# Sample state updates of a GLA decoder step: four masked fp32 matmuls replaced by four single-pass matmuls over stacked halves

## The chip, the cores and the metric

The kernel runs on one core of a Trainium2 chip. The metric is the device time of one execution in microseconds (us). Its engines are PE (matmuls), DVE, ACT and POOL (elementwise work) and SP, which here only issues transfers; ACT issues two as well.

## The reference, cut to what matters

Two layers of a decoder trunk: a half-step SwiGLU FFN, a mixer (gated linear attention beside a convolution, merged by gates), a second FFN. There are 336 token rows: a prompt of 256, 8 running sequences ("samples") of 8 tokens each, 16 meta tokens. The part at hand, for one head (dk = 128, dv = 256) and each of the 8 samples:

```
decay = jnp.exp(b_last[:, :, 0])
upd = jnp.einsum('bnshd,bnshv->bnhdv', k * jnp.exp(b_last - b), v)   # sum over the sample's 8 tokens
S_new = decay[..., None] * S + upd                                    # 128 x 256 per sample and head
```

Everything is float32 outside; large products are made of two fp32r halves ("hi" is the value rounded to fp32r, "lo" the rest).

## The kernel before, in words

All engines follow a hand-written order. The mixer of a layer runs projections, each a block of 8 steps of three matmuls `pgate` (about 3.7 us of PE with nothing between); after each step `tick()` emits one entry of a list `tasks`, so that small pieces of attention stand between the matmuls of the gate blocks. After the task, `tick` calls `fill()`, which emits one step of the depthwise convolution (31 taps for each of 8 channel blocks, one DVE operation on `acc` and one on `acs` a step) when the planner's estimate of DVE's work is more than 7000 ns behind that of PE's. The estimate of a matmul is four times as high for F32 operands as for F32R:

```
clock["pe"] += (n / 2.4 + 2.5) * (4 if b.dtype == F32 else 1)
...
if filler[0] is not None and clock["dve"] + 7000.0 < clock["pe"]:
```

The four heads take a list of 29 slots each (`head_tasks`): `prompt_out` at 0 and 3, `sample_out` at 7 to 13, `sample_state` at 15 and 18 (4 samples each), and at 21 to 23 `head_start` of the next head: scores, `mask_ku` on POOL, then `prompt_state`, whose first part is the update by the 16 meta tokens. What the convolution still owes is emitted at once when the third of the last eight gate blocks begins (`while next(conv, 0)`, block index 2). At the end of that block PE sums the squares of the convolution (`conv_norm_a`, tile `nrm` from `ones_d`), and from that the chain root, reciprocal (`rstd`), scaling, `ch`/`cl` leads to the pointwise projection `pw`.

Keys stand token by token in `kuT` (64 sample tokens in partitions 0 to 63, meta tokens in 64 to 79 of group 2). `mask_ku` writes `km`, eight copies of the keys, each zero outside one sample. `sample_state` then makes four F32 matmuls over 32 rows, two in each of two PSUM banks, and DVE adds them to the decayed state.

SP issues everything in one order: weight pieces `raw` (four buffers, each freed by POOL's or DVE's `wl`), old states `s` (three buffers), new states `out_ss`, prompt states `out_sp`. After each head stand out_ss, load of s, out_ss, load of s; a load of `s` waits until an `out_ss` ahead of it has landed, since it reuses its buffer. All matmuls of PE outside transposes are recorded at L134 (`mm`), nearly all DVE operations at L112.

Of the kernel before, what the change touches and what calls it, by code (L numbers as in the profile page):

```python
# [9 lines left out]
F32 = mybir.dt.float32  # L10
F32R = mybir.dt.float32r
U32 = mybir.dt.uint32
AF = mybir.ActivationFunctionType
ALU = mybir.AluOpType
# [6 lines left out]
NS = 8  # L21
LS = 8
NSAMP = NS * LS
# [6 lines left out]
HEADS = 4  # L30
DK = 128
DV = 256
# [10 lines left out]
NCH = SEQ // CHUNK  # L43
# [74 lines left out]
def trunk_kernel(ctx, tc, wts, x_in, vecs, consts, masks, wdecay, cache, state,  # L118
                 y_out, sp_out, ss_out, u_out):
    nc = tc.nc  # L120
    PE, ACT, POOL, SP = nc.tensor, nc.scalar, nc.gpsimd, nc.sync
# [5 lines left out]
    DVE = Clocked(nc.vector, dve_time)  # L127

    def mm(out, a, b, start, stop):
        n = 1  # L130
        for x in b.shape[1:]:
            n *= x
        clock["pe"] += (n / 2.4 + 2.5) * (4 if b.dtype == F32 else 1)
        PE.matmul(out, a, b, start=start, stop=stop)  # L134
# [21 lines left out]
    seqm = con[:, C_SEQ:C_SEQ + NS]  # L156
# [4 lines left out]
    def bank(name, tag="mm", bufs=4):  # L161
        return psum.tile([128, 512], F32, tag=tag, name=name, bufs=bufs)
# [4 lines left out]
    def grp(g):  # L167
        return slice(g * 128, (g + 1) * 128)
# [174 lines left out]
    def mixer(l, norm, next_block):  # L343
# [6 lines left out]
        gp = gl.enter_context(tc.tile_pool(name="gla", bufs=1, reuse_waits="tile"))  # L350
# [2 lines left out]
        lal = mp.tile([128, 3, 512], F32R, tag="sb", name="lal")  # L353
        qt = gp.tile([128, HEADS, T], F32, name="qt")
        kt = gp.tile([128, HEADS, TP], F32, name="kt")
        kuT = gp.tile([128, 4, HEADS * DK], F32, name="kuT")
        v = gp.tile([128, 3, HEADS * DV], F32, name="v")
        dec = gp.tile([128, HEADS, 2 * NCH + NS], F32, name="dec")
        rT = gp.tile([128, 3], F32, name="rT")
# [16 lines left out]
        ACT.copy(wds[0:64], wdec[0:64])  # L376
        ACT.copy(wdr[64:128], wdec[64:128])
        POOL.tensor_tensor(out=wds[64:128], in0=wdec[64:128], in1=wdr[64:128].bitcast(F32), op=ALU.subtract)
        POOL.memset(kuT[0:64, 3], 0.0)
        cnorm = Norm()  # L380

        ready = [0]
# [149 lines left out]
        at = {0: decay_lr, 6: decay_alr, 14: decay_exp, 18: decay_ln, 70: decay_end}  # L532
# [13 lines left out]
        for hd in range(HEADS):  # L546
# [3 lines left out]
                                     op0=ALU.mult, op1=ALU.mult)  # L550
            DVE.tensor_tensor(out=qt[:, hd, 0:n], in0=pq[:, 0:n], in1=qt[:, hd, 0:n], op=ALU.mult)

        def transposes(hd):
            pt = bank("ptr", "aux", 2)
            for g in range(3):
                PE.transpose(pt[:, grp(g)], ku[:, hd, grp(g)], ident)
                clock["pe"] += 108.0
            hs = slice(hd * DK, (hd + 1) * DK)
            ACT.copy(kuT[:, 0:3, hs], pt[:, :384].rearrange("p (g d) -> p g d", g=3))
            ACT.copy(kuT[64:128, 3, hs], pt[64:128, grp(2)])  # L560

        for hd in range(HEADS):
            pk = bank("pk")
# [25 lines left out]
        hp = gl.enter_context(tc.tile_pool(name="heads", bufs=1, reuse_waits="tile"))  # L589
        s0 = {}  # L590

        def load_s0(i):
            if i < 2 * HEADS:
                t = hp.tile([128, NS // 2, DV], F32, tag="s0", name="s0", bufs=3)
                SP.dma_start(t, state[l, i // 2, i % 2])
                s0[i] = t
# [4 lines left out]
        def scores(hd, st):  # L601
            ps = bank("sc")
            for g in range(3):
                e = min((g + 1) * 128, n)
                mm(ps[:, g * 128:e], kt[:, hd, grp(g)], qt[:, hd, g * 128:e], True, True)
            DVE.copy_predicated(probs[hd % 2].rearrange("p g c -> p (g c)")[:, :n], msk[:, :n], ps[:, :n])

        def prompt_state(hd, st, part):
            ks = slice(hd * DK, (hd + 1) * DK)
            vs = slice(hd * DV, (hd + 1) * DV)  # L610
            pu = bank("upd", "aux", 2)
            if part == 0:
                sp = st["sp"] = hp.tile([128, 2 * NCH, DV], F32, tag="sp", name="sp", bufs=1)
                mm(pu[:, 0:DV], kuT[:, 3, ks], v[:, 2, vs], True, True)
                ACT.activation(sp[:, 0], pu[:, 0:DV], AF.Identity, scale=dec[:, hd, 1:2])
                return
            sp = st["sp"]
            for g in range(NCH):
                mm(pu[:, g * DV:(g + 1) * DV], kuT[:, g, ks], v[:, g, vs], True, True)
            for g in range(NCH):  # L620
                if g:
                    ACT.activation(sp[:, 2 * g], sp[:, 2 * g - 1], AF.Identity, scale=dec[:, hd, 2 * g + 1:2 * g + 2])
                DVE.scalar_tensor_tensor(out=sp[:, 2 * g + 1], in0=sp[:, 2 * g], scalar=dec[:, hd, 2 * g:2 * g + 1],
                                         in1=pu[:, g * DV:(g + 1) * DV], op0=ALU.mult, op1=ALU.add)
            SP.dma_start(sp_out[l, hd], sp[:, 2 * NCH - 1])

        def prompt_out(hd, st, vb):
            sp = st["sp"]
            pr = probs[hd % 2]
            o = st["o", vb] = bank("o")  # L630
            vs = slice(hd * DV + vb * 128, hd * DV + (vb + 1) * 128)
            ss = slice(vb * 128, (vb + 1) * 128)
            for g in range(NCH):
                mm(o[:, grp(g)], v[:, g, vs], pr[:, g], True, False)
                mm(o[:, grp(g)], sp[:, 2 * g, ss], qt[:, hd, grp(g)], False, True)
            mm(o[:, SEQ:n], v[:, 2, vs], pr[:, 2, 0:n - SEQ], True, False)

        def mask_ku(hd, st):
            km = st["km"] = hp.tile([64, NS, DK], F32, tag="km", name="km", bufs=1)
            src = kuT[0:64, 2, hd * DK:(hd + 1) * DK]  # L640
            POOL.tensor_tensor(out=km, in0=src.unsqueeze(1).to_broadcast([64, NS, DK]),
                               in1=seqm[0:64].unsqueeze(2).to_broadcast([64, NS, DK]), op=ALU.mult)

        def sample_out(hd, st, half, vb):
            t = s0[2 * hd + half]
            for i in range(NS // 2):
                s = half * (NS // 2) + i
                cs = slice(SEQ + s * LS, SEQ + (s + 1) * LS)
                mm(st["o", vb][:, cs], t[:, i, vb * 128:(vb + 1) * 128], qt[:, hd, cs], False, s == NS - 1)

        def sample_state(hd, st, p):
            km = st["km"]
            pus = [bank("upds", "aux", 2) for _ in range(2)]
            for e in range(2):
                for half in range(2):
                    s = half * (NS // 2) + 2 * p + e
                    r = slice(32 * half, 32 * half + 32)
                    mm(pus[half][:, e * DV:(e + 1) * DV], km[r, s], v[r, 2, hd * DV:(hd + 1) * DV], True, True)
            for half in range(2):
                t = s0[2 * hd + half]  # L660
                for e in range(2):
                    i = 2 * p + e
                    s = half * (NS // 2) + i
                    DVE.scalar_tensor_tensor(out=t[:, i], in0=t[:, i], scalar=dec[:, hd, 2 * NCH + s:2 * NCH + s + 1],
                                             in1=pus[half][:, e * DV:(e + 1) * DV], op0=ALU.mult, op1=ALU.add)
            if p == 1:
                for half in range(2):
                    SP.dma_start(ss_out[l, hd, half], s0.pop(2 * hd + half))
                    load_s0(2 * hd + half + 3)

        def head_evict(hd, st):
            ot = st["ot"] = hp.tile([128, 2, T], F32, tag="ot", name="ot", bufs=1)
# [17 lines left out]
        hs = [{} for _ in range(HEADS)]  # L690

        def head_start(hd):
            st = hs[hd]
            return {0: lambda: (scores(hd, st), mask_ku(hd, st)), 1: lambda: prompt_state(hd, st, 0),
                    2: lambda: prompt_state(hd, st, 1)}

        def head_tasks(hd):
            st = hs[hd]
            at = {
                0: lambda: prompt_out(hd, st, 0),  # L700
                3: lambda: prompt_out(hd, st, 1),
                7: lambda: sample_out(hd, st, 0, 0),
                9: lambda: sample_out(hd, st, 0, 1),
                11: lambda: sample_out(hd, st, 1, 0),
                13: lambda: (sample_out(hd, st, 1, 1), head_evict(hd, st)),
                15: lambda: sample_state(hd, st, 0),
                18: lambda: sample_state(hd, st, 1),
            }
            if hd:
                at[5] = lambda: head_norm_a(hd - 1, hs[hd - 1])  # L710
                at[10] = lambda: head_norm_b(hd - 1, hs[hd - 1])
            if hd + 1 < HEADS:
                at.update({21 + k: f for k, f in head_start(hd + 1).items()})
            else:
                at[23] = lambda: head_norm_a(hd, st)
                at[28] = lambda: head_norm_b(hd, st)
            return [at.get(k) for k in range(29)]

        at = head_start(0)
# [87 lines left out]
    with tc.manual_schedule():  # L807
# [52 lines left out]
        r = norm.rstd(ones_d, TY)  # L860
        for b in range(KB):
            DVE.scalar_tensor_tensor(out=h[:, b, 0:TY], in0=h[:, b, 0:TY], scalar=vec[:, V_FIN + b:V_FIN + b + 1],
                                     in1=r[:, 0:TY], op0=ALU.mult, op1=ALU.mult)
# [121 lines left out]
```

## Time and profile before

| | |
|---|---|
| median of 3 runs | 1649.36 us (1649.2 to 1652.94) |
| the profiled execution's own time | 1653.15 us |
| its span in the trace | 1651.4 us |
| PE busy | 1615.1 us, 98% |
| DVE, ACT, POOL busy | 65%, 44%, 26% |
| granted PE clock, mean | 0.991 |

The span is what the trace covers, the own time has some 1.8 us around it. Times below are from the start of the span; layer 0's mixer lies at about 255 to 570 us, layer 1's at about 1078 to 1390 us.

### The profile page before, as it was taken

How to read it: one execution, taken by the hardware profiler on the slowest of the kernel's cores; microseconds unless marked ns; L12 is line 12 of the kernel's file. 1: busy time of each engine (PE TensorE's matmuls, PEld its weight loads, DVE VectorE, ACT ScalarE, POOL GpSimd, SP SyncE). 2: the span in 40 equal slices, each digit the busy share in tenths (PEclk: the TensorE clock that was granted, in tenths of full speed). 3: DMA queues.
4: the chain of work that ended last, by engine and by line, in shares of the span. 5: the costliest groups of instructions: out<-in, count | busy, mean ns of one | idle time of the engine just before them, and what ended most of it. 6: DMA issues, size and time to landing. Idle time of an engine off the chain costs nothing.

```text
span 1651.4 us, 27129 instructions
## 1 busy us (share of the span) xinstructions
PE 1615.1 (98%) x10612; PEld 1596.0 (97%) x10612; DVE 1080.0 (65%) x2159; ACT 727.6 (44%) x1154; POOL 424.7 (26%) x284
## 2 busy tenths in 40 slices
PE   8999999899999999999999999998999999999997
PEld 8999999899998999999999999998999989999997
DVE  7666446899986566564456654468998865666543
ACT  5433433743446344333343334347434464433432
POOL 0000016575575310000000000166756652000000
PEclk9999999999999999999999999999999999999999
DMA  5654445365453544444446444553644544445352
GB/s 200 203 181 126 133 152 163 112 182 166 131 173 115 154 140 153 141 130 141 152 142 212 141 134 131 157 150 112 192 156 142 173 136 151 148 153 153 116 171 78
DMA packets 76593, 247.56 MB, mean 150 GB/s; under 512 B 8625, under 2 KB 10929, under 8 KB 76209
## 3 DMA queue, kind: packets, MB, share of 16 engines
q1 hardware_dynamic: 75888, 240.34, 46.3%
q10 hardware_dynamic: 576, 5.49, 0.9%
q8 instruction: 83, 1.36, 0.3%
q14 instruction: 46, 0.37, 0.1%
HBM read 230.08 MB, written 15.71 MB: 149 GB/s over the span
## 4 chain that ended last, share of the span: by engine, by line
PE 85%; DVE 7%; ACT 4%; issue 2%; DMA 1%; POOL 0%; SPq 0%; DVEq 0%; POOLq 0%; ACTq 0%
PE pd L134 19%; PE pu L134 19%; PE pg L134 19%; PE pgate L134 6%; PE pw L134 4%; PE po L134 4%; DVE acc L112 2%; PE pa L134 2%; PE pga L134 2%; PE pv L134 2%; PE o L134 2%; PE pk L134 2%; PE pq L134 2%; DVE acs L112 1%; ACT wh L205 1%
## 5 line engine op out<-in xcount | busy, mean ns | idle before, releaser
L112 DVE TENSOR_TENSOR wl<-raw,wh 128x1024 fp32r<-128x1024 f32 (+1 forms) x320 | 349.3, 1108 | 228.1 <-ACT wh L205 227.6
L205 ACT CAST wh<-raw 128x1024 fp32r<-128x1024 f32 (+3 forms) x456 | 427.7, 956 | 74.4 <-issue 29.4
L207 POOL TENSOR_TENSOR wl<-raw,wh 128x1024 fp32r<-128x1024 f32 (+2 forms) x136 | 308.9, 2285 | 155.1 <-ACT wh L205 146.0
L270 POOL TENSOR_TENSOR ssum<-ssum,sq 128x336 f32<-128x336 f32 (+1 forms) x63 | 56.8, 901 | 1013.9 <-ACT sq L269 1013.8
L112 DVE SCALAR_TENSOR_TENSOR acc<-u,vec,acc 128x272 f32<-128x272 f32 (+1 forms) x480 | 235.2, 490 | 0.0
L134 PE MATMUL pg<-xh,wh 128*128 128x336 f32 (+1 forms) x704 | 222.8, 316 | 6.8 <-ACT wh L205 6.8
L134 PE MATMUL pg<-xh,wl 128*128 128x336 f32 (+1 forms) x704 | 221.8, 315 | 0.3 <-DVE wl L112 0.3
L134 PE MATMUL pu<-xh,wh 128*128 128x336 f32 (+1 forms) x704 | 221.6, 315 | 0.0
L134 PE MATMUL pu<-xh,wl 128*128 128x336 f32 (+1 forms) x704 | 221.6, 315 | 0.0
L134 PE MATMUL pd<-act_hi,wh 128*128 128x336 f32 (+1 forms) x704 | 221.0, 314 | 0.0
L134 PE MATMUL pu<-xl,wh 128*128 128x336 f32 (+1 forms) x704 | 220.9, 314 | 0.0
L134 PE MATMUL pg<-xl,wh 128*128 128x336 f32 (+1 forms) x704 | 220.9, 314 | 0.0
L134 PE MATMUL pd<-act_hi,wl 128*128 128x336 f32 (+1 forms) x704 | 220.3, 313 | 0.0
L134 PE MATMUL pd<-act_lo,wh 128*128 128x336 f32 (+1 forms) x704 | 220.2, 313 | 0.0
L134 PEld LDWEIGHTS pg<-xh,wh 128*128 128x128 f32 x704 | 132.7, 189 | 7.1 <-ACT wh L205 6.8
L112 DVE SCALAR_TENSOR_TENSOR acs<-u,vec,acs 128x64 f32<-128x64 f32 x480 | 135.5, 282 | 0.0
L326 ACT CAST act_hi<-pu 128x336 fp32r<-128x336 f32 (+1 forms) x88 | 38.5, 437 | 217.6 <-DVE pu L112 217.6
L134 PEld LDWEIGHTS pg<-xh,wl 128*128 128x128 f32 x704 | 132.6, 188 | 0.8 <-DVE wl L112 0.8
L134 PEld LDWEIGHTS pg<-xl,wh 128*128 128x128 f32 x704 | 132.7, 188 | 0.4
L134 PEld LDWEIGHTS pu<-xl,wh 128*128 128x128 f32 x704 | 132.6, 188 | 0.0
L134 PEld LDWEIGHTS pu<-xh,wl 128*128 128x128 f32 x704 | 132.6, 188 | 0.0
L134 PEld LDWEIGHTS pu<-xh,wh 128*128 128x128 f32 x704 | 132.6, 188 | 0.0
(200 smaller groups left out, 3277.4 us busy)
## 6 DMA issues: line engine op xcount, KB each, us to landing
raw<-in_wts SPq DMA_DIRECT2D x304, 512.0 KB, 3.6
raw<-in_wts SPq DMA_DIRECT2D x64, 384.0 KB, 3.6
raw<-in_wts SPq DMA_DIRECT2D x64, 320.0 KB, 3.0
s<-in_state SPq DMA_DIRECT2D x16, 512.0 KB, 4.5
out_ss<-s SPq DMA_DIRECT2D x16, 512.0 KB, 5.2
raw<-in_wts SPq DMA_DIRECT2D x16, 344.0 KB, 3.4
u<-in_cache ACTq DMA_DIRECT2D x2, 2424.0 KB, 11.0
out_u<-u SPq DMA_DIRECT2D x16, 303.0 KB, 4.6
```

What stands on the lines that cost most here:

```text
L112: return fn(*args, **kw)
L134: PE.matmul(out, a, b, start=start, stop=stop)
L205: ACT.copy(wh[:, :nk * nw], raw)
L207: eng.tensor_tensor(out=wl[:, :nk * nw], in0=raw, in1=wh[:, :nk * nw].bitcast(F32), op=ALU.subtract)
L270: eng.tensor_tensor(out=self.sum[:, 0:n], in0=self.sum[:, 0:n], in1=sq[:, 0:n], op=ALU.add)
L326: ACT.copy(ah[:, j, 0:n], pu[:, 0:n])
```

## The change: what it does

For each head, `sample_split` casts the head's 64 rows of keys and values to fp32r (`hi`, ACT) and subtracts (`lo`, POOL). `sample_stack` then issues twelve transfers inside SBUF on SP (32 rows of 512 to 1536 bytes, 16 to 48 KB each), which lay the four combinations hi·hi, hi·lo, lo·hi, lo·lo of the 8 tokens of a sample under each other: 32 rows of `kv` per sample, four samples in 128 partitions, two such halves. A sample's update is then one fp32r matmul over 32 rows with 256 columns, in a single pass. `mask_ku` and `km` go. The meta update reads 32 rows of `kuT` group 2 and `v` in place of a zero-padded fourth group of 128 rows, so the fourth group, its memset and its copy go. `head_start` stands one slot earlier (20), and the stacking at slot 25.

```diff
-            ACT.copy(kuT[:, 0:3, hs], pt[:, :384].rearrange("p (g d) -> p g d", g=3))
-            ACT.copy(kuT[64:128, 3, hs], pt[64:128, grp(2)])
+            ACT.copy(kuT[:, :, hs], pt[:, :384].rearrange("p (g d) -> p g d", g=3))
...
-                mm(pu[:, 0:DV], kuT[:, 3, ks], v[:, 2, vs], True, True)
+                mm(pu[:, 0:DV], kuT[NSAMP:NSAMP + 32, 2, ks], v[NSAMP:NSAMP + 32, 2, vs], True, True)
...
-        def mask_ku(hd, st):
-            km = st["km"] = hp.tile([64, NS, DK], F32, tag="km", name="km", bufs=1)
...
+        def sample_split(hd, st):
+            hi = st["hi"] = hp.tile([NSAMP, DK + DV], F32R, tag="hi", name="hi", bufs=1)
+            lo = st["lo"] = hp.tile([NSAMP, DK + DV], F32R, tag="lo", name="lo", bufs=1)
+            for o, w, raw in ((0, DK, kuT), (DK, DV, v)):
+                raw = raw[0:NSAMP, 2, hd * w:(hd + 1) * w]
+                ACT.copy(hi[:, o:o + w], raw)
+                POOL.tensor_tensor(out=lo[:, o:o + w], in0=raw, in1=hi[:, o:o + w].bitcast(F32), op=ALU.subtract)
+
+        def sample_stack(hd, st):
+            dst = st["kv"] = hp.tile([128, 2, DK + DV], F32R, tag="kv", name="kv", bufs=1)
+            hi, lo, ks, vs = st["hi"], st["lo"], slice(0, DK), slice(DK, DK + DV)
+            for r, part in enumerate((((hi, slice(0, DK + DV)),), ((hi, ks), (lo, vs)), ((lo, ks), (hi, vs)),
+                                      ((lo, slice(0, DK + DV)),))):
+                for t, cs in part:
+                    for e in range(2):
+                        SP.dma_start(dst[r:128:4, e, cs].bitcast(F32), t[32 * e:32 * e + 32, cs].bitcast(F32))
...
-                for half in range(2):
-                    s = half * (NS // 2) + 2 * p + e
-                    r = slice(32 * half, 32 * half + 32)
-                    mm(pus[half][:, e * DV:(e + 1) * DV], km[r, s], v[r, 2, hd * DV:(hd + 1) * DV], True, True)
...
+                for j in range(2):
+                    r = slice(32 * (2 * p + j), 32 * (2 * p + j) + 32)
+                    mm(pus[j][:, e * DV:(e + 1) * DV], st["kv"][r, e, 0:DK], st["kv"][r, e, DK:], True, True)
...
-            return {0: lambda: (scores(hd, st), mask_ku(hd, st)), 1: lambda: prompt_state(hd, st, 0),
+            return {0: lambda: (scores(hd, st), sample_split(hd, st)), 5: lambda: sample_stack(hd, st), 1: lambda: prompt_state(hd, st, 0),
...
-                at.update({21 + k: f for k, f in head_start(hd + 1).items()})
+                at.update({20 + k: f for k, f in head_start(hd + 1).items()})
```

SP's order in layer 0, from the second state store after head 1 to the weight pieces that follow (`s` are state buffers). Before:

```order
L668 DMA out_ss<-s_4510 128x1024
L595 DMA s_4775<-in_state 128x1024
L625 DMA out_sp<-sp 128x256
L192 DMA raw_4847<-in_wts 128x1024
L192 DMA raw_4906<-in_wts 128x1024
```

The same place now:

```order
L675 DMA out_ss<-s_4520 128x1024
L593 DMA s_4790<-in_state 128x1024
L623 DMA out_sp<-sp 128x256
L651 DMA kv<-hi 32x384 x2
L651 DMA kv<-hi 32x128 x2
L651 DMA kv<-lo 32x256 x2
L651 DMA kv<-lo 32x128 x2
L651 DMA kv<-hi 32x256 x2
L651 DMA kv<-lo 32x384 x2
L192 DMA raw_4865<-in_wts 128x1024
```

The twelve transfers of head 2's `kv` stand behind head 2's out_sp, and that behind the stores and loads of head 1's states.

DVE's order in layer 0 after the 18th eviction of the mixer (`pgate`, block index 1 of the last eight): head 3's reciprocal and output `ot`, then the convolution's reciprocal and its scaling `u`. Before:

```order
L112 TENSOR_TENSOR pgate<-pgate,rstd 128x336
L112 RECIPROCAL rstd<-sd 128x336
L112 SCALAR_TENSOR_TENSOR ot<-ot,vec,rstd 128x336 x2
L112 TENSOR_TENSOR pgate<-pgate,rstd 128x336
L112 RECIPROCAL rstd<-sd 128x336
L112 SCALAR_TENSOR_TENSOR u<-u,vec,rstd 128x336
```

Now, from the last step of the convolution on:

```order
L112 SCALAR_TENSOR_TENSOR acc<-u,vec,acc 128x272
L112 SCALAR_TENSOR_TENSOR acs<-u,vec,acs 128x64
L112 RECIPROCAL rstd<-sd 128x336
L112 SCALAR_TENSOR_TENSOR ot<-ot,vec,rstd 128x336 x2
L112 TENSOR_TENSOR pgate<-pgate,rstd 128x336
L112 RECIPROCAL rstd<-sd 128x336
L112 SCALAR_TENSOR_TENSOR u<-u,vec,rstd 128x336
```

In all, 18 rows (nine steps) of the convolution now stand between the 18th eviction and head 3's reciprocal, in layer 1 14 rows (seven steps); before, none in either layer. In layer 0 thirteen steps have moved from ahead of the 16th eviction to behind it.

## Rows read from the trace of the kernel before

**Rows 1.** Waits of PE: line waited for: us in total, times, longest us.

```profile
PE pw L134 <- DVE cl L112: 4.0, 2, 2.0
PE pw L134 <- ACT ch L747: 3.2, 2, 1.9
```

**Rows 2.** Timeline of PE, 420.7 to 422.6 us: start, us, line, operation, out<-in.

```profile
420.81 0.32 PE L134 MATMUL pgate<-xl,wh 128*128 128x336 f32 x1
420.96 0.32 PE L134 MATMUL pgate<-xh,wl 128*128 128x336 f32 x1
421.21 1.13 PE L134 MATMUL upds<-v,km 32*128 32x256 f32 x8
...
422.53 0.32 PE L134 MATMUL pgate<-xl,wh 128*128 128x336 f32 x1
```

**Rows 3.** Timeline of PE, 403 to 406 us, the meta update of head 0.

```profile
403.27 0.32 PE L134 MATMUL pgate<-xh,wl 128*128 128x336 f32 x1
403.42 0.59 PE L134 MATMUL upd<-v,kuT 128*128 128x256 f32 x2
...
404.00 0.32 PE L134 MATMUL pgate<-xl,wh 128*128 128x336 f32 x1
```

**Rows 4.** Groups by line, POOL: busy us, mean ns, idle before and its releaser.

```profile
L641 POOL TENSOR_TENSOR km<-kuT,con 64x1024 f32<-64x1024 f32 x8 | 15.2, 1895 | 0.2
```

**Rows 5.** Timeline of SP's queue, layer 0, 436 to 467 us.

```profile
437.49 0.38 SPq L625 DMA_DIRECT2D out_sp<-sp  x1
...
466.32 0.33 SPq L595 DMA_DIRECT2D s<-in_state  x1
466.74 0.38 SPq L625 DMA_DIRECT2D out_sp<-sp  x1
```

**Rows 6.** Timeline of SP's queue, layer 1, 1255 to 1292 us.

```profile
1261.62 0.38 SPq L625 DMA_DIRECT2D out_sp<-sp  x1
...
1287.89 0.38 SPq L625 DMA_DIRECT2D out_sp<-sp  x1
```

**Rows 7.** Timeline of PE: first sample_state call of heads 1 and 2, both layers.

```profile
445.63 1.13 PE L134 MATMUL upds<-v,km 32*128 32x256 f32 x8
...
470.59 1.13 PE L134 MATMUL upds<-v,km 32*128 32x256 f32 x8
...
1267.79 1.13 PE L134 MATMUL upds<-v,km 32*128 32x256 f32 x8
...
1291.67 1.13 PE L134 MATMUL upds<-v,km 32*128 32x256 f32 x8
```

**Rows 8.** Transfers: line, operation, count, KB each, median us from issue to landing.

```profile
out_y<-h SPq DMA_DIRECT2D x8, 160.0 KB, 1.9
out_sp<-sp SPq DMA_DIRECT2D x8, 128.0 KB, 4.9
```

**Rows 9.** Timeline of DVE, 476 to 545 us: last convolution steps, a later eviction.

```profile
488.11 0.50 DVE L112 SCALAR_TENSOR_TENSOR acc<-u,vec,acc 128x272 f32<-128x272 f32 x1
...
488.71 0.50 DVE L112 SCALAR_TENSOR_TENSOR acc<-u,vec,acc 128x272 f32<-128x272 f32 x1
...
501.62 0.52 DVE L112 TENSOR_TENSOR pgate<-pgate,rstd 128x336 f32<-128x336 f32 x1 [1.15 <-PE pgate L134]
```

**Rows 10.** Timeline of POOL, 476 to 545 us: last sum of squares of the convolution.

```profile
490.40 0.91 POOL L270 TENSOR_TENSOR ssum<-ssum,sq 128x336 f32<-128x336 f32 x1 [1.26 <-ACT sq L269]
```

**Rows 11.** Timeline of PE: the norm sums of head 3 and of the convolution.

```profile
501.35 0.73 PE L134 MATMUL nrm<-ssum,ones_v 128*128 128x336 f32 x2
...
505.60 0.73 PE L134 MATMUL nrm<-ssum,ones_d 128*128 128x336 f32 x2
...
1321.80 0.70 PE L134 MATMUL nrm<-ssum,ones_v 128*128 128x320 f32 x2
...
1325.86 0.70 PE L134 MATMUL nrm<-ssum,ones_d 128*128 128x320 f32 x2
```

**Rows 12.** Busy time in one stretch: length, PE, PEld, DVE, ACT, POOL, PEclk, DMA.

```profile
528.20:535.00 6.80, 6.05 (x22) 6.06 (x23) 4.04 (x9) 3.64 (x7) 2.00 (x2) 0.50 0.26 77
```

More of the change, by code (lines that the diff above doesn't have):

```diff
@@ L355, in mixer @@
         kt = gp.tile([128, HEADS, TP], F32, name="kt")
-        kuT = gp.tile([128, 4, HEADS * DK], F32, name="kuT")
+        kuT = gp.tile([128, 3, HEADS * DK], F32, name="kuT")
         v = gp.tile([128, 3, HEADS * DV], F32, name="v")
@@ L378, in mixer @@
         POOL.tensor_tensor(out=wds[64:128], in0=wdec[64:128], in1=wdr[64:128].bitcast(F32), op=ALU.subtract)
-        POOL.memset(kuT[0:64, 3], 0.0)
         cnorm = Norm()
@@ L636, in prompt_out @@
             mm(o[:, SEQ:n], v[:, 2, vs], pr[:, 2, 0:n - SEQ], True, False)
-        def mask_ku(hd, st):
-            km = st["km"] = hp.tile([64, NS, DK], F32, tag="km", name="km", bufs=1)
-            src = kuT[0:64, 2, hd * DK:(hd + 1) * DK]
-            POOL.tensor_tensor(out=km, in0=src.unsqueeze(1).to_broadcast([64, NS, DK]),
-                               in1=seqm[0:64].unsqueeze(2).to_broadcast([64, NS, DK]), op=ALU.mult)
+        def sample_split(hd, st):
[13 more added lines that the diff above has]
+                        SP.dma_start(dst[r:128:4, e, cs].bitcast(F32), t[32 * e:32 * e + 32, cs].bitcast(F32))
         def sample_out(hd, st, half, vb):
@@ L651, in sample_state @@
         def sample_state(hd, st, p):
-            km = st["km"]
             pus = [bank("upds", "aux", 2) for _ in range(2)]
             for e in range(2):
-                for half in range(2):
-                    s = half * (NS // 2) + 2 * p + e
-                    r = slice(32 * half, 32 * half + 32)
-                    mm(pus[half][:, e * DV:(e + 1) * DV], km[r, s], v[r, 2, hd * DV:(hd + 1) * DV], True, True)
-            for half in range(2):
-                t = s0[2 * hd + half]
-                for e in range(2):
[L662 to L665, printed above, removed]
+                for j in range(2):
+                    r = slice(32 * (2 * p + j), 32 * (2 * p + j) + 32)
+                    mm(pus[j][:, e * DV:(e + 1) * DV], st["kv"][r, e, 0:DK], st["kv"][r, e, DK:], True, True)
+            for j in range(2):
+                for e in range(2):
+                    i = 2 * p + j
+                    c = 2 * NCH + e * (NS // 2) + i
+                    t = s0[2 * hd + e]
+                    DVE.scalar_tensor_tensor(out=t[:, i], in0=t[:, i], scalar=dec[:, hd, c:c + 1],
+                                             in1=pus[j][:, e * DV:(e + 1) * DV], op0=ALU.mult, op1=ALU.add)
             if p == 1:
-                for half in range(2):
-                    SP.dma_start(ss_out[l, hd, half], s0.pop(2 * hd + half))
-                    load_s0(2 * hd + half + 3)
+                for e in range(2):
+                    SP.dma_start(ss_out[l, hd, e], s0.pop(2 * hd + e))
+                    load_s0(2 * hd + e + 3)
         def head_evict(hd, st):
```

## The prediction

> **What bounds the kernel now.** I read the shares of busy time first: PE works in 98% of the span (the table above), so what PE executes, and what keeps it waiting, sets the time. Then the list of PE's waits: in both mixers it waits at the pointwise projection for the convolution's halves, 7.2 us together [rows 1]; behind that wait its clock stands at 0.50, the 1.2 GHz level, for 6.8 us in layer 0 [rows 12]. No wait of PE's list is for `km` or an earlier stage of attention. So a PE matmul that goes is worth its time, until PE has to wait for something else. Then the timelines of PE, SP and DVE around the places that the change moves.
>
> **What PE saves.** A plain single-pass matmul of 336 columns follows the one before in 0.15 us (420.81 to 420.96) [rows 2]; 256 columns are then 0.117 us. A whole F32 matmul of 256 columns costs 0.42 us: 404.00 less 403.27 less two plain ones [rows 3]. One call of `sample_state` costs 422.53 − 420.96 − 0.31 = 1.26 us [rows 2]. Four F32 matmuls one behind another would be 1.70; so the two row groups overlap in pairs, 0.85 us, and 0.41 us goes for the change of shape at both ends. With single passes the call costs 0.41 + 2 × 0.117 = 0.64 us if the pairs still overlap (0.62 saved), 0.88 if they don't (0.38 saved, the weight loads then being no longer behind a long stream). There are 16 calls: 6.1 to 9.9 us, I take the middle, **−8.0 us**. Against it, the meta update has still 256 F32 columns, but over 32 rows: it pays a change of shape like that of a call, from nothing to 0.41 us each, eight of them: 0 to 3.3, I take the middle, **+1.6 us**.
>
> **What ACT and POOL get.** POOL loses `km`, 1.9 us a head [rows 4], and gets two subtractions with 384 elements a partition instead of 1024, an estimated 0.7 us. ACT loses a copy and gets two casts with as many elements, an estimated 0.7 us. They lie beside gate work, ACT at 44% and POOL at 26% busy, and I cost them at nothing. Without that cover they delay the prompt state's scaling behind them on ACT, and `prompt_out` on PE, by at most these 0.7 us a head, 5.6 us in all; the slot gained (0.46 us) takes most of it back, so I leave it out.
>
> **The twelve transfers.** This is the disputed part. `kv` of a head is issued behind its out_sp, and that behind the state stores and loads of the head before it. In the trace out_sp of head 1 leaves at 437.49 and its first call is on PE at 445.63, 8.1 us later; for head 2 it is 466.74 and 470.59, only 3.9 us [rows 5, 7]. In layer 1 it is 6.2 us (1261.62 to 1267.79) and 3.8 us (1287.89 to 1291.67) [rows 6, 7]. Nothing on PE depends on out_sp before, so this costs nothing; now six of the transfers must have landed for the call's first matmul, and the others for its third. SP's next issue comes 0.42 us after one that waits for nothing (466.32 to 466.74) [rows 5]; I take 0.45. The last of twelve leaves 5.4 us after out_sp. It lands 1.9 us (a plain store with nothing bulky behind it) to 4.9 us (out_sp, with a state load ahead of it) later [rows 8]; the new ones are small and the last of them has mostly small ones ahead, so 1.9. Needed: 7.3 us after out_sp. PE comes 0.3 us earlier by the saving in the preceding call (0.5, less 0.2 for the meta update). For the head-2 gaps I take 1 us off, since DVE has fewer convolution steps ahead of the states that SP waits to store. PE then waits 7.3 + 0.3 − 3.9 − 1 = 2.7 us for head 2 of layer 0, 2.8 in layer 1, 1.4 for head 1 of layer 1, and not for head 1 of layer 0 (7.6 against 8.1): **+7.0 us**. With 4.9 us for landing it is 18.5; with 3 us off the head-2 gaps, 3. Heads 0 and 3 have more room, since out_sp leaves earlier there. Weight pieces queued behind the twelve are some 5 us later; the four raw buffers and the four pieces already split cover that.
>
> If each transfer had to wait for the one ahead, 1.9 us each [rows 8], a head would need 12 × 1.9 = 22.8 us, and heads 1 and 2 of both layers alone would hold PE for 4 × 22.8 − (8.1 + 3.9 + 6.2 + 3.8) = 69 us: about 1719 us. SP's rows show an issue 0.42 us after another whose transfer cannot have landed by then [rows 5], so I read the landing as paid once, and give this serial case 2 in 100. The Trainium skill ("DMA: Bandwidth & Descriptors", Rules for kernel authors) speaks against this change in that way: small transfers are to be coalesced, since under 64 KB one pays mostly overhead, and the page's fixed cost is 2.0 us for each. By that rule taken twelve times over, the estimate would be some 1723 us.
>
> **The convolution that is late.** The planner counts the new matmuls at a quarter, so `fill` gives out fewer convolution steps, and nine of them (layer 1: seven) now stand on DVE behind the 18th eviction. A step takes 0.60 us (488.11 to 488.71) [rows 9]. DVE waits for PE at that eviction (501.62, 0.27 us after head 3's norm sum starts at 501.35) [rows 9, 11], so it cannot start earlier. The steps end at 501.62 + 0.4 + 5.4 = 507.4. From the end of a block's last step (488.71 + 0.60 = 489.3) to that of its sum of squares on POOL (490.40 + 0.91) it takes 2.0 us by ACT and POOL [rows 9, 10]: 509.4. PE wants that sum at 505.60 [rows 11] and waits **+3.8 us**. In layer 1 the eviction by the same distance is at 1322.1, the sum is there at 1322.1 + 0.4 + 4.2 + 2.0 = 1328.7, wanted at 1325.86 [rows 11]: **+2.8 us**. Nothing hides this: what follows on PE needs the same order, and the chain to `pw` starts at that sum. Its bounds are 5.5 to 8.
>
> **The clock.** After the waits at `pw` PE ran 22 matmuls in 6.05 us at the 1.2 GHz level [rows 12]; at 0.15 us each they would have taken 3.4, so that stretch lost 2.7. A wait of nearly 3 us may bring the like. After the convolution's sum it would only shorten the wait at `pw`, which hangs on DVE and ACT; after the two head-2 waits it would be lost: 0 to 5.4, I take **+3 us**.
>
> **Sum.** −8.0 + 1.6 + 7.0 + 6.6 + 3 = +10.2 us on the profiled execution (1653.15), whose own time is 3.8 above the median; I apply it to the median of 1649.36: 1659.6, **1660 us**.
>
> **The rivals.**
> The transfers land in time. For it: DVE could be further ahead, and head 1 of layer 0 has room already; against it, 3.9 us of room must hold twelve issues of 0.42. Then −8.0 + 1.6 + 6.6 = +0.2: 1650 us, no change.
> The landing is slow (4.9 us) and the clock falls each time: −8.0 + 1.6 + 18.5 + 6.6 + 5.4 = +24: 1673 us.
> Faster: the 0.41 us at the ends of a call belongs to the four-pass form. Then a call costs 0.23 and 16 of them save 16.4 us, with nothing extra for the meta update. It decides if the transfers cost their lower bound: −16.4 + 3 + 6.6 = −7: 1642 us. Against it: the ends show where PE's shape changes, which stays.
>
> **How the numbers follow.** The forecast (1654.5 to 1668) has 0.54; slow landing or the serial reading 0.16 (0.02 of it serial); no change 0.18; faster 0.12. A measurement of this kernel can tell 0.3% (5 us) from no change. So slower 0.70, same 0.18, faster 0.12. The range from 1646 to 1673 leaves out most of the faster case and the slow tail; the forecast's own is 1654.5 to 1668.
>
> **What would show it.** Calls of `upds` at 0.64 to 0.88 us; a wait of PE for the transfers at the first `upds` of head 2 in both layers, 2 to 4 us; a wait of PE at `nrm` from `ones_d` for POOL's sum, near 3.8 and 2.8 us. I am wrong if PE's list of waits lacks either, or if its clock falls more than twice anew.

## The result and the profile after

The changed kernel takes 1671.53 us (1669.99 to 1673.13, 4 runs) against 1650.14 us (1649.2 to 1652.94, 4 runs) of the kernel before: 1.0128 times as long, 95% interval 1.0115 to 1.0140, 21.4 us more. Its profiled execution took 1671.56 us, the span is 1669.8 us, the granted clock 0.987; span against span it is 18.4 us more. The other 3 us are in the comparison: the profiled execution of before lay 3 us above the median of its kernel, and the forecast put a sum made on it against the median.

The list of PE's waits of the changed kernel (line waited for: us in total, times, longest us):

```profile
...
PE upds L134 <- DMA kv<-lo: 8.2, 4, 3.2
...
PE nrm L134 <- POOL ssum L270: 6.4, 2, 3.8
PE pw L134 <- DVE cl L112: 4.0, 2, 2.0
PE upds L134 <- issue: 3.5, 1, 3.5
PE pw L134 <- ACT ch L754: 2.7, 2, 1.9
```

Three rows are new: `upds` for `kv`, 8.2 us, `upds` for "issue", 3.5, and `nrm` for POOL's sum, 6.4; `pw` stays near what it was, 6.7 us in place of 7.2 [rows 1]. The 3.5 us are head 2 of layer 0, and it is `kv` too, as PE's timeline and SP's queue show together:

```profile
474.49 0.32 PE L134 MATMUL pgate<-xh,wl 128*128 128x336 f32 x1
478.29 1.29 PE L134 MATMUL upds<-kv 32*128 32x256 f32 x4 [3.48 <-issue]
```

```profile
438.48 0.38 SPq L623 DMA_DIRECT2D out_sp<-sp  x1
438.96 0.38 SPq L192 DMA_DIRECT2D raw<-in_wts  x1
439.43 2.39 SPq L651 DMA_DIRECT2D kv<-hi  x4
441.87 3.55 SPq L651 DMA_DIRECT2D kv<-lo  x4
445.46 1.23 SPq L651 DMA_DIRECT2D kv<-hi  x2
446.73 1.23 SPq L651 DMA_DIRECT2D kv<-lo  x2
...
456.86 0.38 SPq L675 DMA_DIRECT2D out_ss<-s  x1
462.23 0.33 SPq L593 DMA_DIRECT2D s<-in_state  x1
...
469.16 0.38 SPq L623 DMA_DIRECT2D out_sp<-sp  x1
469.64 2.42 SPq L651 DMA_DIRECT2D kv<-hi  x4
472.16 2.46 SPq L651 DMA_DIRECT2D kv<-lo  x4
474.66 1.41 SPq L651 DMA_DIRECT2D kv<-hi  x2
476.12 1.22 SPq L651 DMA_DIRECT2D kv<-lo  x2
```

Head 2's twelve issues run from 469.64 to 477.34, 0.64 us each, and the call starts at 478.29. Its first matmul needs the six transfers of the first half, of which the eleventh issue is the last; that began at 476.12, 2.2 us ahead of the call, and a transfer of its kind lands 2.0 us after its issue (count, KB each, median us from issue to landing):

```profile
kv<-lo SPq DMA_DIRECT2D x16, 48.0 KB, 2.0
```

The issues are what is long (one takes 0.59 us at the median for a transfer of 32 rows, against 0.33 to 0.38 us for the 128-row ones beside them). For head 1, whose out_sp left at 438.48, they end at 447.96, 0.71 each on average, and the call is at 448.86, after a wait of 3.0 us:

```profile
448.86 1.14 PE L134 MATMUL upds<-kv 32*128 32x256 f32 x4 [2.99 <-DMA kv<-lo]
```

Layer 1 has the same, first on PE, then on SP:

```profile
1278.90 0.38 PE L134 MATMUL upds<-kv 32*128 32x256 f32 x2 [1.73 <-DMA kv<-lo]
...
1306.86 0.89 PE L134 MATMUL upds<-kv 32*128 32x256 f32 x4 [3.17 <-DMA kv<-lo]
```

```profile
1269.29 0.37 SPq L623 DMA_DIRECT2D out_sp<-sp  x1
...
1297.88 0.38 SPq L623 DMA_DIRECT2D out_sp<-sp  x1
```

What PE executes got shorter and longer as the shapes changed. First a call of `sample_state`, then the meta update (one F32 matmul is two records, so x2):

```profile
421.99 0.32 PE L134 MATMUL pgate<-xh,wl 128*128 128x336 f32 x1
422.23 0.50 PE L134 MATMUL upds<-kv 32*128 32x256 f32 x4
...
422.92 0.32 PE L134 MATMUL pgate<-xl,wh 128*128 128x336 f32 x1
```

```profile
403.90 0.32 PE L134 MATMUL pgate<-xh,wl 128*128 128x336 f32 x1
404.15 0.69 PE L134 MATMUL upd<-v,kuT 32*128 32x256 f32 x2
...
405.04 0.31 PE L134 MATMUL pgate<-xl,wh 128*128 128x336 f32 x1
```

Reckoned as in the prediction, the call costs 422.92 − 421.99 − 0.31 = 0.62 us, against 1.26 [rows 2], and the calls that wait for nothing save 0.62 to 0.64, 0.63 on average; the meta update 405.04 − 403.90 − 0.31 = 0.83, against 0.42 [rows 3].

The clock fell to 0.50 behind all four waits for `kv` of more than 1 us and behind the wait at `nrm` of layer 0 (3.8 us), but not behind that of layer 1 (2.6 us). These are the new stretches at that level (length, PE, PEld, DVE, ACT, POOL, PEclk, DMA), with the sum of all eight:

```profile
...
447.46:454.29 6.83, 5.43 (x20) 4.38 (x21) 2.88 (x7) 3.46 (x8) 2.24 (x5) 0.50 0.53 171
478.18:485.01 6.83, 6.59 (x24) 5.55 (x25) 3.31 (x8) 3.64 (x9) 5.30 (x6) 0.50 0.68 227
519.14:522.55 3.41, 3.41 (x14) 3.41 (x14) 3.38 (x4) 3.37 (x5) 3.11 (x3) 0.50 0.01 2
...
1280.32:1283.73 3.41, 3.41 (x15) 2.85 (x14) 2.38 (x7) 2.06 (x5) 1.98 (x3) 0.50 0.67 245
1307.62:1311.03 3.41, 3.41 (x15) 2.87 (x13) 1.65 (x4) 0.09 (x1) 2.38 (x5) 0.50 0.91 334
...
sum 37.54, PE 34.52 PEld 31.33 DVE 24.41 ACT 20.33 POOL 19.45; mean PE 4.31 PEld 3.92 DVE 3.05 ACT 2.54 POOL 2.43
```

The sum of the four of before:

```profile
sum 23.90, PE 20.40 PEld 20.41 DVE 18.53 ACT 15.74 POOL 10.20; mean PE 5.10 PEld 5.10 DVE 4.63 ACT 3.93 POOL 2.55
```

PE works 34.5 us in eight stretches at the 1.2 GHz level, 20.4 us in four before ([rows 12] is one of the four). What the lower level costs can be read from plain matmuls of 336 columns, which follow each other in 0.28 us there (480.24 to 480.52 on PE's timeline, in the second of these stretches) and in 0.15 us at 2.4 GHz [rows 2]. So an estimated (34.5 − 20.4) × (1 − 0.15/0.28) = 6.5 us are lost anew. That is a balance: the four stretches behind the waits for `kv` alone hold 18.8 us of PE's work, but the one behind `pw` in layer 0 is 3.4 us long in place of 6.8, and that at 1129 us of before, ahead of layer 1's sample updates, has no counterpart in this execution. The account of the span: 17.5 us more of PE waits (the lists sum to 44.0 and 26.5), calls −10.1 (16 × 0.63), meta updates +3.3, clock +6.5: 17.2 of 18.4 us.

### The profile page after: what moved, and what is told of

The parts are those of the page before. It is cut to its first block, busy times and chain, and to the rows that moved or that the text cites. A ratio compares the mean times of both kernels' runs of the same rounds, so it can differ in the third digit from the quotient of the medians.

```text
span 1669.8 us, 27179 instructions
## 1 busy us (share of the span) xinstructions
PE 1615.5 (97%) x10548; PEld 1593.3 (95%) x10548; DVE 1081.8 (65%) x2159; ACT 729.4 (44%) x1162; POOL 417.1 (25%) x290
## 4 chain that ended last, share of the span: by engine, by line
PE 84%; DVE 8%; ACT 4%; DMA 2%; issue 1%; SPq 1%; POOL 0%; DVEq 0%; ACTq 0%; POOLq 0%
PE pg L134 19%; PE pu L134 19%; PE pd L134 19%; PE pgate L134 6%; PE pw L134 4%; PE po L134 3%; DVE acc L112 3%; PE pa L134 2%; PE pga L134 2%; PE pv L134 2%; PE pk L134 2%; PE pq L134 2%; DVE acs L112 1%; PE o L134 1%; DVE u L112 1%
## 5 line engine op out<-in xcount | busy, mean ns | idle before, releaser
L134 PE MATMUL pgate<-xh,wh 128*128 128x336 f32 (+1 forms) x384 | 135.2, 352 | 0.0
```

## The experiments

The theory: SP's place in line and its issue time make `kv` late, the planner's count makes the convolution late, and the clock falls behind most of these waits. The main rival for the transfers: it is their landing, or what the fabric does with them. Unless said otherwise each kernel is the changed one with the edit shown; times are medians, before stands at 1650.1 to 1650.7 us beside them.

**The planner's count as before.**

```diff
                     mm(pus[j][:, e * DV:(e + 1) * DV], st["kv"][r, e, 0:DK], st["kv"][r, e, DK:], True, True)
+                    clock["pe"] += 3 * (DV / 2.4 + 2.5)
```

> Only the planner's count is changed back: each of the new sample matmuls counts as much PE time as the F32 one did, so the convolution's steps stand where they stood before the change and none is left for DVE behind the 18th eviction. Theory (the convolution that is late costs its own waits): PE's two waits at nrm for POOL's sum (4.1 and 2.9 us of gap) go, and the time falls by 6 to 9 us against the changed kernel, to about 1664; PE's waits for kv stay at 10 to 14 us, since DVE has convolution steps ahead of the states again. Rival (the waits only move): the chain to pw or the transfers swallow it, nrm's waits go and pw's or kv's grow by as much, and the time stays within 2 us of 1671.5.

1666.21 us, ratio to before 1.0088 [1.0073, 1.0103]: 5.3 us less.

```profile
PE upds L134 <- DMA kv<-lo: 9.6, 5, 4.2
...
PE upds L134 <- issue: 3.4, 1, 3.4
...
PE nrm L134 <- DVE ssum L112: 1.2, 1, 1.2
...
PE nrm L134 <- POOL ssum L270: 0.5, 1, 0.5
```

`nrm`'s wait for POOL's sum goes from 6.4 to 0.5 us, so the late convolution is shown. The gain is a little under the 6 to 9 expected, since 1.3 us come back at `kv` (13.0 in all), 1.2 at `pw` and 1.2 at `nrm` for DVE's sum.

**Half of the transfers.**

```diff
-                    for e in range(2):
+                    for e in range(1):
                         SP.dma_start(dst[r:128:4, e, cs].bitcast(F32), t[32 * e:32 * e + 32, cs].bitcast(F32))
...
-                    mm(pus[j][:, e * DV:(e + 1) * DV], st["kv"][r, e, 0:DK], st["kv"][r, e, DK:], True, True)
+                    mm(pus[j][:, e * DV:(e + 1) * DV], st["kv"][r, 0, 0:DK], st["kv"][r, 0, DK:], True, True)
```

> Leaves out half of the stacking: six of the twelve transfers of a head are issued (those of the first half of the samples), and both halves of the updates read that one stack; matmuls, casts and order stay. Theory (what PE waits for is SP's issuing, 0.64 to 0.71 us a transfer): six fewer issues take 3.8 to 4.3 us off each of the waits of 3.3, 3.8, 2.0 and 3.5 us at heads 1 and 2, so PE's waits for kv are under 1 us in all, and with the clock the time is 1650 to 1657. Rival (it is the landing of the last transfer, whatever stands ahead): the waits shrink by less than 1 us each and the time is above 1665.

1659.58 us, 1.0054 [1.0037, 1.0071]: 12 us less, between the two expectations. Waits at `upds` are 4.5 us, not under 1. In the timelines head 2 of layer 0 has `kv` 5.8 us after out_sp (465.84 to 471.68) where it was 9.1: six issues less are 3.3 us less, 0.55 each, a little under the 0.64 to 0.71 of the theory. What I had left out is that PE, no longer held at head 1, is ready at head 2 sooner (471.68 less the wait of 1.7 is 4.2 us after out_sp, where it had been 5.7). So the wait is shortened by less than the issues.

**The transfers on two queues.**

```diff
-                        SP.dma_start(dst[r:128:4, e, cs].bitcast(F32), t[32 * e:32 * e + 32, cs].bitcast(F32))
+                        (ACT if e else SP).dma_start(dst[r:128:4, e, cs].bitcast(F32), t[32 * e:32 * e + 32, cs].bitcast(F32))
```

> Only the six transfers of the second half of the samples are issued by ACT instead of SP; both engines issue their six at the same slot, nothing is left out. Theory (issuing on one queue is what PE waits for): the waits for kv fall to 3 to 5 us in all, as in the run with half the transfers, and the time is 1657 to 1663, if ACT's other work isn't late. Rival (landing, or the fabric's time for twelve transfers): kv waits stay above 8 us and the time above 1667.

1659.94 us (one of the four runs took 1653.68), 1.0051 [1.0031, 1.0072], with waits of 5.0 us at `upds`:

```profile
PE upds L134 <- DMA kv<-lo: 3.5, 2, 2.5
...
PE upds L134 <- DVE ot L112: 1.5, 1, 1.5
```

The row that names `ot` is a wait for `kv` too, here as in the run before: nothing of a call needs `ot`, and in the kernel before the change a call starts at 445.63 [rows 7] while `ot` is written until 447.4. All twelve transfers are made, and the time is that of half of them; an issue takes 0.58 to 0.61 us at the median on either queue, as it did on the one. So it is not the landing or the fabric's time for twelve transfers that PE waits for; what two queues share out is the issuing. The Trainium skill ("DMA: Bandwidth & Descriptors", Rules for kernel authors) says that spreading transfers over engines saves sequencer issue time only; the run agrees, and here that time, with the clock, was worth 11.6 us.

**The transfers ahead of the state stores.** The split of head h+1 goes to slot 12 of head h; `head_start` keeps split and stack for head 0 alone.

```diff
             if p == 1:
+                if hd + 1 < HEADS:
+                    sample_stack(hd + 1, hs[hd + 1])
                 for e in range(2):
                     SP.dma_start(ss_out[l, hd, e], s0.pop(2 * hd + e))
...
+                at[12] = lambda: sample_split(hd + 1, hs[hd + 1])
```

> The split of head h+1 stands at slot 12 of head h, and its twelve transfers stand on SP ahead of the state stores of head h (behind the last sample matmuls of head h) instead of behind the stores, the state loads and out_sp. The transfers are the same in number, size and queue. Theory (SP's order makes them late): PE's waits for kv, 11.8 us, go, with the half-clock stretches right behind them (20.5 us at 0.5, so up to 10 us of loss); the time falls to 1650 to 1656. Rival (the transfers themselves are slow, by landing or by what they take from other transfers): waits for kv of more than 5 us remain and the time is above 1662. Second rival: the state loads, now 8 us later, are late for sample_out; then o waits for s by 1 to 4 us a head, and the time is 1658 to 1670.

1669.63 us, 1.0112 [1.0097, 1.0127]: 1.9 us less. The theory's 1650 to 1656 is missed, and the second rival holds:

```profile
PE o L134 <- DMA s<-in_state: 7.8, 3, 4.8
```

No wait for `kv` is left, and the state loads, behind 7.7 us of issues, are late in its place; the longest wait, 4.8 us, goes with 13.7 us at the lower clock. What stands on SP behind the twelve issues is late by them.

**The transfers between stores and loads.** The split stays at slot 12, but six of the transfers stand behind each of the two stores.

```diff
                 for e in range(2):
                     SP.dma_start(ss_out[l, hd, e], s0.pop(2 * hd + e))
+                    if hd + 1 < HEADS:
+                        sample_stack(hd + 1, hs[hd + 1], e)
                     load_s0(2 * hd + e + 3)
```

> As in the run with the transfers ahead of the state stores, the split of head h+1 stands at slot 12 of head h; but six of its transfers now stand behind the first state store of head h and six behind the second, each ahead of the state load that waits for that store to land (5.4 us in the changed kernel). Theory (SP's order, and its time spent waiting for stores to land): the issues fit into that waiting, so the waits for kv (11.8 us) go and the state loads come no later than before; o doesn't wait for s; the nrm waits (6.4 us) stay; with the clock the time is 1650 to 1657. Rival (transfers and state loads can't both be in time on one queue): o waits for s by 3 us or more in all, or kv is still waited for, and the time is above 1660.

1653.41 us (10 runs), 1.0017 [1.0008, 1.0026]: 18.1 us less than the changed kernel, with the same twelve transfers of the same size on the same queue.

```profile
454.15 0.72 SPq L676 DMA_DIRECT2D out_ss<-s  x1
454.96 1.62 SPq L652 DMA_DIRECT2D kv<-hi  x2
456.64 1.23 SPq L652 DMA_DIRECT2D kv<-lo  x2
457.91 0.59 SPq L652 DMA_DIRECT2D kv<-hi  x1
458.55 0.59 SPq L652 DMA_DIRECT2D kv<-lo  x1
459.24 0.89 SPq L593 DMA_DIRECT2D s<-in_state  x1
460.17 0.43 SPq L676 DMA_DIRECT2D out_ss<-s  x1
```

From store to load there are 5.1 us now, 5.4 before the edit: the load waited for the store to land, and the six issues fit into that. In PE's list no wait for `kv` or `s` is left; all its waits sum to 32.4 us, 11.6 less, and PE's work at the lower clock is 22.0 us, 12.5 less, an estimated 5.8 us. Together 17.4 of the 18.1 us.

**The meta update alone.** 128 zero-padded rows again, by the lines of the diff of the change put back.

> Only the meta update is put back to 128 zero-padded rows (fourth group of kuT, its memset and its copy back; hi and lo share one tile to make room). Theory: the update costs 0.42 us again in place of 0.82, eight times 0.40 = 3.2 us of PE; where PE then waits for kv anyway (heads 1 and 2 of both layers) the 0.4 goes into the wait, so the time falls by 1.6 to 3.2 us, to 1668 to 1670. Rival (the 32-row form costs nothing by itself, the change of shape is paid elsewhere): the time stays within 1 us.

1670.74 us, 1.0119 [1.0103, 1.0134]: 0.8 us less, not to be told from the rival. The updates are at 0.38 us a record again, but `kv` waits grow by 0.7 us and there are more stretches at the lower clock. Inconclusive, so it was repeated where nothing waits for `kv`.

**All three edits**: between stores and loads, the planner's count, the meta update as before.

> The run with the transfers between the stores and loads, and with it the planner's count as before the change and the meta update over 128 zero-padded rows. Theory: what is left of the change is the shorter calls, 16 times 0.63 us = 10 us of PE, with no wait for kv, s or at nrm and no more half-clock stretches than before the change; the time is 1637 to 1645 against 1650.4 of the kernel before. Rival (with the calls shorter something else on DVE or SP becomes late, so that PE's waits come back elsewhere): 1648 to 1656.

**And the same with the meta update over 32 rows:**

> The run with the transfers between the stores and loads and the planner's count as before, but with the meta update over 32 rows, as the change has it. Against the run with all three, only the meta update differs, and PE has no wait for kv that could swallow it. Theory (0.82 in place of 0.42 us for each of eight updates): 3.2 us more, 1649 to 1651. Rival (the run with the meta update alone showed 0.8 us, and that is its price): 1646 to 1648.

1646.63 us (9 runs), 0.9976 [0.9966, 0.9986], and 1648.35 us (11 runs), 0.9988 [0.9979, 0.9997]. The meta update is worth 1.7 us, between both expectations: PE's busy time differs by 2.5 us, and part of it had been waited for anyway. With all three edits the kernel beats the one before the change by 3.9 us, but it lies between the expected 1637 to 1645 and the rival's 1648 to 1656. PE is busy for 1605.5 us, 9.6 less than before; its waits have grown by 3.6, though (the lists sum to 30.1 and 26.5), and span against span it is 5.9 us shorter, the profiled execution of before having been 2.6 us above the median of its kernel:

```profile
PE upds L134 <- DVE s L112: 2.1, 4, 1.0
...
PE nrm L134 <- POOL ssum L270: 1.2, 1, 1.2
```

PE now comes to the second call before DVE has added the states of the first (which frees the bank), and to the convolution's sum before that is made.

**The convolution further ahead**: as with all three, `clock["pe"] += 6 * (DV / 2.4 + 2.5)`.

> The run with all three, but each sample matmul counts for seven times its columns instead of four in the planner, so that more convolution steps stand ahead of the last eight gate blocks. Theory (what keeps PE waiting now is DVE with the convolution, 1.2 us at nrm, and 2.1 us at upds where DVE adds the states): the nrm wait goes and the upds waits stay, 1 to 2 us less, 1644 to 1646. Rival (the steps ahead of the state sums make PE wait at upds, or SP's stores and the loads late): 1647 to 1652.

1652.91 us, 1.0019 [1.0010, 1.0027], 6.3 us more than with all three: my theory fell, and the rival's first half holds, just above its 1647 to 1652. The `nrm` wait for POOL went, but the steps ahead of the state sums cost more at `upds`:

```profile
PE upds L134 <- DVE s L112: 6.6, 8, 2.2
```

## Why the prediction was off

The direction was as forecast, and so were the two kinds of wait, for `kv` and at `nrm`, in all their places but one (head 1 of layer 0). The time lies in the wide range (1646 to 1673), but above the forecast's own (1654.5 to 1668): of 21 us measured 10 were forecast. Step by step, the runs price the changed kernel's parts one after another (1671.53 to 1653.41, 1648.35, 1646.63, and 1650.54 before):

| part | forecast | measured |
|---|---|---|
| transfers, with the clock | +7.0 + 3 | +18.1 |
| late convolution | +3.8 + 2.8 | +5.1 |
| meta update | +1.6 | +1.7 |
| calls, with what waits for them | −8.0 | −3.9 |

**The term that failed is that of the twelve transfers, with its clock.** The step took 0.45 us an issue, from a 128-row load of a state and the store behind it [rows 5]; the new transfers took 0.64 to 0.71. That made 9.0 to 10.4 us from out_sp to the call in the four cases, not 7.3. The landing, 2.0 us, was taken well at 1.9, and the room before the call was 5.7 and 5.8 us at head 2 where I had 4.6 and 4.5. Heads 2 were thus forecast nearly right (2.7 and 2.8 us; 3.5 and 3.2), by two errors that partly offset each other, and so was head 1 of layer 1 (1.4 us; 2.0), where the room was 7.9 us in place of 5.9. Head 1 of layer 0, costed at nothing with 0.5 us to spare, waited 3.0 us (its room was 7.4 us): there the longer issues and a weight piece ahead of them ate the margin. Waits of 11.7 us in place of 7.0 are 4.7 of the missing 8.1.

**The clock** was taken at about one stretch like that of [rows 12], behind the waits of the heads 2; in fact all four long waits for `kv` were followed by one. The prediction itself named a clock that falls more than twice anew as a sign of being wrong. By the estimates above it cost 6.5 us in place of 3 against before, 5.8 by the run between stores and loads: 2.8 more of the missing 8.1.

The rival that named 1673 us comes nearest in number, half of it by luck. It has the landing of the last transfer at 4.9 us, and that was 2.0; its other half, a clock that falls each time, came true.

**What PE saves** was right in its bounds: 0.63 us a call, the upper one (I took the middle), and 0.41 us more for a meta update, the upper one too. The faster rival, with 0.23 us left of a call, is out: it is 0.62. That +1.6 for the meta updates meets the measured +1.7 is luck: eight of them cost PE 3.3 us, and part of that goes into waits. PE's busy time says −9.6 us for the calls. That the calls give back only 3.9 of it, even with all else mended, I had not seen: after them DVE's sums and the convolution are late. In the changed kernel itself PE waited for `kv` there, so its list has no such row at `upds`.

**The late convolution** held: `nrm` waited 6.4 us where 6.6 was forecast, and with the planner's count put back the time falls by 5.1 to 5.3.

The serial reading, by which each transfer waits for the one ahead, is out: at head 2 of layer 0 the call starts 8.7 us after the first is issued, not twelve times 1.9. The Trainium skill's rule that spoke for it ("DMA: Bandwidth & Descriptors", Rules for kernel authors: coalesce what is under 64 KB) points the right way, but the overhead that was paid twelve times here is the issue of each, not the landing. Another rule of that section of the Trainium skill, that the setup cost of a transfer issued early overlaps with compute, agrees with the run between stores and loads, in which no wait for `kv` is left.

Not settled: what of a call's saving could be kept if the DVE sums were ordered anew, and why these transfers take longer to issue than the 128-row ones: they have fewer rows, write every fourth partition and stay inside the on-chip memory, and no run separates these.

## What to carry to other kernels

Cost a transfer's issue by a row of the same shape, and where a margin is as near to zero as head 1's, cost the case in which it is gone; twelve small transfers hold a queue for nearly 8 us. Look in the queue for the time it already spends waiting (here a load for the landing of a store) and put the new issues there. Price a wait of PE with the stretch at the lower clock behind it, and a planner that is told of less PE work with the work that it then hands out late.

## What the runs showed of the hardware

A transfer of 32 rows inside the on-chip memory took 0.59 us to issue on SP at the median, stores and loads of 128 rows mostly 0.33 to 0.38 us. An F32 matmul over 32 rows between matmuls over 128 cost 0.83 us where the one over 128 rows cost 0.42, for the same 256 columns. In the changed kernel waits of PE of 1.7 to 3.5 us for `kv` each went with 3.4 or 6.8 us at the 1.2 GHz level, and in the run with the transfers ahead of the state stores one of 4.8 us for `s` went with 13.7. It is no rule: a wait of 2.6 us at `nrm` in the changed kernel, and one of 1.7 us for `kv` in the run with half the transfers, had no such stretch behind them.
